# Where the transposes before the last gate stand, which PSUM banks its first token tiles take, and which queue issues the last store

## The chip, the cores and the metric

The kernel runs on one core of one Trainium2 chip. A core has TensorE (PE; its weight loads are listed as PEld), VectorE (DVE), ScalarE (ACT), GpSimd (POOL) and SyncE (SP), which run side by side and wait for each other by semaphores. SP, ACT and POOL also issue DMAs. The metric is the device time of one execution in microseconds (us). It is compared between the kernel before and the kernel after the change.

## What is computed

The reference is one layer of a hybrid decoder trunk over 512 tokens of width 1024, all in float32. The change touches only its last line but one and its last line, the gate on the per-layer embedding and the final norm:

```python
x = x + conv_ffn(rmsnorm(x, ffn_norm), ...)
gate = sigmoid(rmsnorm(x, ple_norm) @ w_ple_gate)     # 512x1024 @ 1024x1024
x = x + gate * (p @ w_ple)
return rmsnorm(x, final_norm)
```

## The kernel before, in words

**Arithmetic.** Each float32 product is made of three matmuls: an operand is split into a high and a low part (`split_into`, L239 on ScalarE and L240 on VectorE; weights by `parts`, L68 on ScalarE and L69 on VectorE), and `mm3` (L204, L205, L206) adds high by high, high by low and low by high into one PSUM bank.

**PSUM.** A bank holds 128 x 512 floats. There are five rotating banks, which the trace calls `mm` (`bank()`), two fixed ones, `sd` (`seeded`), and one small one. A rotating bank is handed out again in the same circular order; whoever gets it waits until its earlier holder has been read for the last time.

**The end of the kernel.** The feed-forward part ends with a down projection (`seven`). While its last steps run on TensorE, some other work is put among them by a list of fillers: the transposes of the second token half (`turn(1, k)`) and products of the embedding with `w_ple` into one `mm` bank, both `sd` banks and another `mm` bank, which ScalarE copies out (L650).

`turn(th, k)` takes one rotating bank, transposes four 128 x 128 blocks of the residual `x` into it on TensorE (L691), and splits the result, scaled by the norm's gain, into an `xe` tile (two instructions L239 on ScalarE, two L240 on VectorE). Four turns make the left operand for the gate of one token half, 256 tokens.

Then the gate loop (L764 on) goes over the four tiles of 128 tokens in the order 2, 3, 0, 1. Tiles 2 and 3 are the second token half, tiles 0 and 1 the first. A tile has 8 steps over the width `k`, each with two groups of three matmuls, one for each half of 512 output columns: 48 matmuls of 512 columns. When its banks are full, sigmoid (L788, in place in the bank), multiply (L789), add (L790), square with row sum (L791, also into the bank) and multiply by the final gain (L792) follow for each half, on ScalarE and VectorE; then the row scale (`rstd_1`, a power on GpSimd at L613), the scaling (L800 on VectorE; for the last half of the last tile L798 on ScalarE) and two stores (L801), all issued by SP. The last tile, 1, is cut into one group of 512 and two of 256 columns.

The gate's weights `wg` are split at the same time as tile 2 runs. Before tile 3, all four turns of the first token half stand in the program text:

```python
for b in (2, 3, 0, 1):
    th, j = divmod(b, 2)
    last = b == 1
    if b == 3:
        for k in range(HK):
            turn(0, k)
```

The scheduler that lays out the instructions of each engine can move an instruction ahead of others; what it made of this text is shown with the change.

Of the kernel before, what the change touches and what calls it, by code (L numbers as in the profile page):

```python
# [14 lines left out]
T = 512  # L15
# [15 lines left out]
HK = KD // 2  # L31
# [13 lines left out]
def trunk(ctx, tc, xT, xr, pT, wsT, par, bsp, w_u0, w_u1, w_v, w_ga, w_gb, w_p, w_pl,  # L45
          w_a, w_b, w_o, w_up, w_dn, w_g, w_ple, gfin, out):
    nc = tc.nc
# [11 lines left out]
    def block(name, shape=(2, T), dtype=F32):  # L59
        return blk.tile([P, *shape], dtype, tag="blk", name=name)  # L60
# [141 lines left out]
    def mm3(o, w, a, first, last, **kw):  # L202
        (wh, wl), (ah, al) = w, a
        PE.matmul(o, wh, ah, start=first, stop=False, **kw)  # L204
        PE.matmul(o, wh, al, start=False, stop=False, **kw)  # L205
        PE.matmul(o, wl, ah, start=False, stop=last, **kw)  # L206
# [10 lines left out]
    def bank():  # L217
        return ps.tile([P, T], F32, tag="mm", name="mm")
# [9 lines left out]
    def split(src, scale=None):  # L228

        b = block("blk", (2, T), F32R)  # L230
        split_into(b, src, scale)
        return b

    def split_into(b, src, scale=None):
        if scale is None:
            S.copy(b[:, 0, :], src)
            V.tensor_tensor(b[:, 1, :], src, b[:, 0, :].bitcast(F32), op=ALU.subtract)  # L237
        else:
            S.activation(b[:, 0, :], src, AF.Copy, scale=scale)  # L239
            V.scalar_tensor_tensor(b[:, 1, :], src, scale, b[:, 0, :].bitcast(F32),  # L240
                                   op0=ALU.mult, op1=ALU.subtract)
# [9 lines left out]
    def col(c, i):  # L251
        return pr[:, c + i:c + i + 1]
# [69 lines left out]
    seeded = [psb.tile([P, T], F32, tag=f"sd{n}", name="sd") for n in range(2)]  # L322
# [123 lines left out]
    for k in range(KD):  # L446
        if k + 1 < KD:
            load(k + 1)
        b = split(x[k], col(C_MIX, k))
# [23 lines left out]
    for f in range(KD):  # L473
# [4 lines left out]
        if f % 2:  # L478
            k = f // 2
# [126 lines left out]
    def rstd_1(sums):  # L606

        ms = small.tile([P, 1], F32, tag="fms", name="fms", bufs=NT)
        V.tensor_scalar(ms, sums[0], 1.0 / D, EPS, op0=ALU.mult, op1=ALU.add)
        for s in sums[1:]:  # L610
            V.scalar_tensor_tensor(ms, s, 1.0 / D, ms, op0=ALU.mult, op1=ALU.add)
        r = small.tile([P, 1], F32, tag="fr", name="fr", bufs=8)
        G.tensor_tensor(r, ms, neghalf[:, :1], op=ALU.pow)  # L613
        return r
# [5 lines left out]
    def columns(z, b, f):  # L620

        return z[b][:, f // HK, f % HK * P:(f % HK + 1) * P]
# [43 lines left out]
    def conv(i, o):  # L666
        cc = work("cc")
        S.activation(cc, o, AF.Identity, scale=col(C_CW, 3 * i + 2), bias=col(C_CB, i))
        V.scalar_tensor_tensor(cc[:, 1:], o[:, :T - 1], col(C_CW, 3 * i + 1), cc[:, 1:],
                               op0=ALU.mult, op1=ALU.add)  # L670
        V.scalar_tensor_tensor(cc[:, 2:], o[:, :T - 2], col(C_CW, 3 * i), cc[:, 2:],
                               op0=ALU.mult, op1=ALU.add)
        return cc
# [12 lines left out]
    def turn(th, k):  # L686
        tp = bank()
        t = block("xe", (2, 2, H), F32R)
        for i, f in enumerate((k, HK + k)):
            for j in range(2):  # L690
                PE.transpose(tp[:, (2 * i + j) * P:(2 * i + j + 1) * P], columns(x, 2 * th + j, f), ident)  # L691
        for i, f in enumerate((k, HK + k)):
            split_into(t[:, i], tp[:, i * H:(i + 1) * H], col(C_PLE, f))
        XE[th].append(t)
# [23 lines left out]
    for i in range(KF):  # L718
# [11 lines left out]
        b = conv(2 * i + 1, o2)  # L730
# [13 lines left out]
        if part:  # L744
            q0, n = part
            last = q0 + n == KF // 2
# [17 lines left out]
    for b in (2, 3, 0, 1):  # L764
        th, j = divmod(b, 2)
        last = b == 1
        if b == 3:
            for k in range(HK):
                turn(0, k)

        if last:
            groups = [[(bank(), 0)], [(bank()[:, :H], T)], [(bank()[:, :H], T + H)]]
        else:
            groups = [[(bank(), 0), (bank(), T)]]
        fss = small.tile([P, 3], F32, tag="fss", name="fss")
        n = 0
        for group in groups:
            for k in range(KD):
                a = XE[th][k % HK][:, k // HK]
                a = [a[:, z, j * P:(j + 1) * P] for z in range(2)]  # L780
                for ob, c0 in group:
                    mm3(ob, a, [z[:, c0:c0 + ob.shape[-1]] for z in wg[k]], k == 0, k == KD - 1)
            for ob, c0 in group:
                w = ob.shape[-1]
                fh, c1 = divmod(c0, T)
                pc = ple[b][:, fh, c1:c1 + w]
                xc = x[b][:, fh, c1:c1 + w]
                S.activation(ob, ob, AF.Sigmoid, scale=r_emb[b])  # L788
                V.tensor_tensor(pc, ob, pc, op=ALU.mult)  # L789
                V.tensor_tensor(xc, xc, pc, op=ALU.add)  # L790
                S.activation(ob, xc, AF.Square, accum_out=fss[:, n:n + 1])  # L791
                V.tensor_tensor(pc, xc, gB[:, c0:c0 + w], op=ALU.mult)  # L792
                n += 1
        r = rstd_1([fss[:, i:i + 1] for i in range(n)])
        for g in range(2):
            ot = ple[b][:, g]
            if g and last:
                S.activation(ot, ot, AF.Copy, scale=r)  # L798
            else:
                V.tensor_scalar_mul(ot, ot, r)  # L800
            nc.sync.dma_start(out[b, :, g * T:(g + 1) * T], ot)  # L801


_ORDER = ["xT", "xr", "pT", "wsT", "par", "bsp", "w_u0", "w_u1", "w_v", "w_ga", "w_gb", "w_p", "w_pl",
# [72 lines left out]
```

## Time and profile before

| what | value |
|---|---|
| time, median of 3 runs | 784.43 us (784.0 to 787.2) |
| the profiled execution: its time | 783.97 us |
| its span in the trace | 782.2 us |
| TensorE busy | 770.5 us, 98% of the span |
| VectorE, ScalarE, GpSimd busy | 532.2, 376.8, 59.9 us |
| chain of work that ended last | TensorE 95% of the span |

The profiled execution's time is 1.77 us more than its span, since the span begins and ends with the first and last instruction in the trace. Times in the trace count from the span's start. L numbers are lines of the kernel before.

### The profile page before, as it was taken

The numbers are of one execution on the slowest core, as the hardware profiler recorded it, in microseconds if no ns is written. First come the engines' busy times: TensorE is split into PE (matmuls) and PEld (weight loads), VectorE is DVE, ScalarE is ACT, GpSimd is POOL, SyncE is SP. The second block draws the span as 40 slices with busy tenths as digits, with TensorE's granted clock in tenths as the row PEclk, the third lists the DMA queues.
The fourth block names the chain that finished last, engine by engine and source line by source line (L and its number), as shares of the span: only waits on it lengthen the run. The fifth ranks groups of instructions, "written<-read, shape, count | busy, mean of one in ns | idle before, by whom it ended". The sixth has DMA issues, their size and how long they took to land.

```text
span 782.2 us, 9301 instructions
## 1 busy us (share of the span) xinstructions
PE 770.5 (98%) x3482; PEld 639.4 (82%) x3482; DVE 532.2 (68%) x748; ACT 376.8 (48%) x542; POOL 59.9 (8%) x97
## 2 busy tenths in 40 slices
PE   9999999999999999999999999999999999999896
PEld 8888878888888888888888888888888888888785
DVE  7795668766566734636576778666668767679735
ACT  5576765582232312325545454544445534458713
POOL 0310200000112100001000000000001010030300
PEclk9999999999999999999999999999999999999998
DMA  9992624224032508101831444732335572383211
GB/s 339 325 229 93 176 81 136 107 97 171 30 109 80 215 27 311 67 0 57 323 113 46 108 108 108 274 131 54 81 109 134 203 196 58 108 185 98 81 54 54
DMA packets 40925, 103.21 MB, mean 132 GB/s; under 512 B 3632, under 2 KB 3760, under 8 KB 40880
## 3 DMA queue, kind: packets, MB, share of 16 engines
q1 hardware_dynamic: 33280, 86.78, 31.9%
q0 software_dynamic: 6016, 11.54, 9.0%
q10 hardware_dynamic: 1584, 4.31, 1.5%
q8 instruction: 27, 0.44, 0.2%
q14 instruction: 18, 0.15, 0.1%
HBM read 99.46 MB, written 3.15 MB: 131 GB/s over the span
## 4 chain that ended last, share of the span: by engine, by line
PE 95%; DVE 2%; DMA 1%; ACT 1%; issue 1%; POOLq 0%; ACTq 0%; DVEq 0%
PE mm L204 25%; PE mm L205 25%; PE mm L206 25%; PE sd L204 6%; PE sd L205 6%; PE sd L206 6%; DMA pt<-in_pT 1%; PE mm L515 1%; PE wake L261 1%; PE mm L628 0%; PE mm L691 0%; ACT whi L68 0%; DVE wlo L69 0%; DVE sg L590 0%; DVE sg L589 0%
## 5 line engine op out<-in xcount | busy, mean ns | idle before, releaser
L69 DVE TENSOR_TENSOR wlo<-raw,whi 128x1024 fp32r<-128x1024 f32 (+1 forms) x186 | 217.9, 1178 | 158.9 <-ACT whi L68 158.4
L68 ACT CAST whi<-raw 128x1024 fp32r<-128x1024 f32 (+1 forms) x179 | 183.8, 1031 | 203.3 <-PE mm L206 59.8
L204 PE MATMUL mm<-blk,whi 128*128 128x512 f32 x480 | 187.3, 391 | 0.0
L205 PE MATMUL mm<-blk,whi 128*128 128x512 f32 x480 | 187.1, 390 | 0.0
L206 PE MATMUL mm<-blk,wlo 128*128 128x512 f32 x480 | 186.6, 389 | 0.0
L204 PEld LDWEIGHTS mm<-blk,whi 128*128 128x128 f32 x480 | 90.3, 188 | 19.1 <-DVE blk L240 0.2
L206 PEld LDWEIGHTS mm<-blk,wlo 128*128 128x128 f32 x480 | 90.2, 188 | 18.8
L205 PEld LDWEIGHTS mm<-blk,whi 128*128 128x128 f32 x480 | 90.3, 188 | 18.5
L204 PE MATMUL mm<-whi,blk 128*128 128x512 f32 x210 | 82.1, 391 | 0.0
L205 PE MATMUL mm<-wlo,blk 128*128 128x512 f32 x210 | 81.8, 389 | 0.0
L206 PE MATMUL mm<-whi,blk 128*128 128x512 f32 x210 | 81.7, 389 | 0.0
L204 PEld LDWEIGHTS mm<-whi,blk 128*128 128x128 f32 x210 | 39.4, 188 | 8.3 <-DVE blk L237 0.2
L206 PEld LDWEIGHTS mm<-whi,blk 128*128 128x128 f32 x210 | 39.4, 188 | 8.2
L205 PEld LDWEIGHTS mm<-wlo,blk 128*128 128x128 f32 x210 | 39.4, 188 | 8.0
L204 PE MATMUL sd<-whi,blk 128*128 128x512 f32 x114 | 44.5, 391 | 0.0
L206 PE MATMUL sd<-whi,blk 128*128 128x512 f32 x114 | 44.4, 389 | 0.0
L205 PE MATMUL sd<-wlo,blk 128*128 128x512 f32 x114 | 44.4, 389 | 0.0
L105 POOL DMA_DIRECT2D raw<-in_w_dn x16 | 18.2, 1241 | 314.9 <-DMA raw<-in_w_dn 205.1
L204 PE MATMUL sd<-whi,cmb 128*128 128x512 f32 x92 | 36.0, 391 | 0.8 <-ACT u L375 0.8
L204 PE MATMUL mm<-whi,cmb 128*128 128x512 f32 x92 | 36.1, 392 | 0.0
L205 PE MATMUL sd<-wlo,cmb 128*128 128x512 f32 x92 | 35.8, 389 | 0.0
L206 PE MATMUL mm<-whi,cmb 128*128 128x512 f32 x92 | 35.8, 389 | 0.0
(171 smaller groups left out, 1080.8 us busy)
## 6 DMA issues: line engine op xcount, KB each, us to landing
raw<-in_w_up SPq DMA_DIRECT2D x44, 512.0 KB, 4.5
raw<-in_w_dn SPq DMA_DIRECT2D x25, 512.0 KB, 3.6
raw<-in_w_dn POOLq DMA_DIRECT2D x12, 512.0 KB, 6.3
raw<-in_w_v SPq DMA_DIRECT2D x10, 512.0 KB, 9.7
raw<-in_w_ga SPq DMA_DIRECT2D x10, 512.0 KB, 4.1
raw<-in_w_gb SPq DMA_DIRECT2D x8, 512.0 KB, 3.6
raw<-in_w_p SPq DMA_DIRECT2D x8, 512.0 KB, 4.5
raw<-in_w_b SPq DMA_DIRECT2D x8, 512.0 KB, 3.9
```

The source lines that it names most:

```text
L68: (V.tensor_copy if first else S.copy)(hi[:, :cols], raw[:, :cols])
L69: V.tensor_tensor(lo[:, :cols], raw[:, :cols], hi[:, :cols].bitcast(F32), op=ALU.subtract)
L105: (G if kw else nc.sync).dma_start(o, block_of(name, ch), **kw)
L204: PE.matmul(o, wh, ah, start=first, stop=False, **kw)
L205: PE.matmul(o, wh, al, start=False, stop=False, **kw)
L206: PE.matmul(o, wl, ah, start=False, stop=last, **kw)
L261: PE.matmul(wake, ones, ones, start=True, stop=True)
L515: PE.matmul(mx[:, n * P:(n + 1) * P], vt[n].rearrange("p a t -> p (a t)")[:, f * P:(f + 1) * P], wsm[:, f, :], start=True, stop=True)
```

## The change

Three things are changed. The four turns of the first token half no longer stand between tile 2 and tile 3; each is written behind one of tile 2's last four steps (`k` = 4 to 7). The first tile of each half (2 and 0, `j == 0`) takes the two `sd` banks and not two rotating ones. And the very last store, the second half of tile 1, is issued by ScalarE, which also makes that half's data, and not by SP. Above the diff's first line everything is as before; from L767 on the lines of the kernel after are lower by up to three (L788 becomes L787, L801 becomes L800).

```diff
     for b in (2, 3, 0, 1):
         th, j = divmod(b, 2)
         last = b == 1
-        if b == 3:
-            for k in range(HK):
-                turn(0, k)
 
         if last:
             groups = [[(bank(), 0)], [(bank()[:, :H], T)], [(bank()[:, :H], T + H)]]
         else:
-            groups = [[(bank(), 0), (bank(), T)]]
+            groups = [[(seeded[0], 0), (seeded[1], T)] if j == 0 else [(bank(), 0), (bank(), T)]]
...
         for group in groups:
...
                 for ob, c0 in group:
                     mm3(ob, a, [z[:, c0:c0 + ob.shape[-1]] for z in wg[k]], k == 0, k == KD - 1)
+                if b == 2 and k >= HK:
+                    turn(0, k - HK)
...
-            nc.sync.dma_start(out[b, :, g * T:(g + 1) * T], ot)
+            (nc.scalar if g and last else nc.sync).dma_start(out[b, :, g * T:(g + 1) * T], ot)
```

On TensorE, the end of tile 2 and the start of tile 3 before the change (`mm<-...,xe` are gate matmuls, `mm<-ident,x` transposes):

```order
L204 MATMUL mm<-whi,xe 128x512 x2
L205 MATMUL mm<-wlo,xe 128x512
L206 MATMUL mm<-whi,xe 128x512
L205 MATMUL mm<-wlo,xe 128x512
L206 MATMUL mm<-whi,xe 128x512
L691 MATMUL mm<-ident,x 128x128 x13
L204 MATMUL mm<-whi,xe 128x512
```

Three of the sixteen transposes had already been moved ahead, into step 3 of tile 2, and stay there in both kernels; the other thirteen stood in one row between the tiles. The same place after the change, from step 6 of tile 2 on:

```order
L691 MATMUL mm<-ident,x 128x128 x4
L204 MATMUL sd<-whi,xe 128x512
L205 MATMUL sd<-wlo,xe 128x512
L206 MATMUL sd<-whi,xe 128x512
L204 MATMUL sd<-whi,xe 128x512
L205 MATMUL sd<-wlo,xe 128x512
L206 MATMUL sd<-whi,xe 128x512
L691 MATMUL mm<-ident,x 128x128 x4
L204 MATMUL mm<-whi,xe 128x512
```

Tile 2 now fills `sd` banks, and the thirteen stand as 1, 4, 4 and 4 behind its steps 4, 5, 6 and 7; tile 3 starts behind the last four.

On ScalarE, from the last weight split on, before the change (the `ACT_TABLE_LOAD` is the one for sigmoid):

```order
L68 CAST whi<-raw 128x1024
L788 ACT_TABLE_LOAD
L788 ACTIVATE mm<-mm,fr 128x512 x2
L239 ACTIVATE xe<-mm,pr 128x256 x3
L791 ACTIVATE mm,fss<-x 128x512 x2
L239 ACTIVATE xe<-mm,pr 128x256 x5
L788 ACTIVATE mm<-mm,fr 128x512 x2
```

And after it:

```order
L239 ACTIVATE xe<-mm,pr 128x256 x5
L787 ACT_TABLE_LOAD
L787 ACTIVATE sd<-sd,fr 128x512
L239 ACTIVATE xe<-mm,pr 128x256 x2
L787 ACTIVATE sd<-sd,fr 128x512
L239 ACTIVATE xe<-mm,pr 128x256
L790 ACTIVATE sd,fss<-x 128x512 x2
L787 ACTIVATE mm<-mm,fr 128x512 x2
```

Most splits of the turned tiles now stand ahead of tile 2's sigmoids; there is one table load in both.

## Rows read from the trace of the kernel before

**Rows 1.** The page: the span, and the granted TensorE clock in 40 slices.

```profile
span 782.2 us, 9301 instructions
...
PEclk9999999999999999999999999999999999999998
```

**Rows 2.** The chain that ended last, 735 to 740 us: start, length, what.

```profile
735.83 0.24 PE mm L206
736.10 0.67 ACT mm L788
...
738.77 0.73 ACT mm L791 x2
739.54 0.66 PE mm L691 x4
```

**Rows 3.** Timeline of TensorE, tiles 2 and 3: start, length, engine, line.

```profile
725.11 0.39 PE L204 MATMUL mm<-whi,xe 128*128 128x512 f32 x1
...
736.35 1.14 PE L691 MATMUL mm<-ident,x 128*128 128x128 f32 x9
739.54 0.66 PE L691 MATMUL mm<-ident,x 128*128 128x128 f32 x4 [2.05 <-ACT mm L791]
740.16 0.50 PE L204 MATMUL mm<-whi,xe 128*128 128x512 f32 x1
...
743.72 0.58 PE L204 MATMUL mm<-whi,xe 128*128 128x512 f32 x1
...
744.37 0.40 PE L206 MATMUL mm<-whi,xe 128*128 128x512 f32 x1
```

**Rows 4.** Three stretches: length, each engine's busy time, granted clock, DMA share, GB/s.

```profile
716.36:720.09 3.73, 3.73 (x25) 3.22 (x24) 3.52 (x10) 2.62 (x7) 0.00 (x0) 1.00 0.00 0
...
736.35:740.16 3.81, 1.76 (x15) 1.32 (x13) 3.31 (x6) 3.44 (x9) 0.00 (x0) 1.00 0.23 83
740.16:744.37 4.21, 4.21 (x12) 3.30 (x12) 3.74 (x11) 1.91 (x5) 0.54 (x1) 0.59 0.30 118
```

**Rows 5.** Timeline of TensorE, two places with transposes among matmuls.

```profile
716.36 1.03 PE L691 MATMUL mm<-ident,x 128*128 128x128 f32 x8
...
717.70 0.39 PE L206 MATMUL mm<-whi,cmb 128*128 128x512 f32 x1
...
729.64 0.49 PE L691 MATMUL mm<-ident,x 128*128 128x128 f32 x3
...
730.90 0.40 PE L204 MATMUL mm<-whi,xe 128*128 128x512 f32 x1
```

**Rows 6.** Instructions that write the turned tiles `xe`: ns min/median/max, first and last start.

```profile
L239 ACT ACTIVATE xe<-mm,pr x16: 471/474/491, 717.0 to 744.3; 128x256 fp32r<-128x256 f32 x16
L240 DVE SCALAR_TENSOR_TENSOR xe<-mm,pr,xe x16: 470/476/484, 717.5 to 744.8; 128x256 fp32r<-128x256 f32 x16
```

**Rows 7.** Timeline of VectorE during tile 2.

```profile
728.16 5.76 DVE L69 TENSOR_TENSOR wlo<-raw,whi 128x1024 fp32r<-128x1024 f32 x5 [0.78 <-ACT whi L68]
```

**Rows 8.** Timeline of ScalarE just before tile 2.

```profile
723.22 1.31 ACT L650 COPY ple<-sd 128x512 f32<-128x512 f32 x2
```

**Rows 9.** Timeline of all engines at the end.

```profile
777.86 0.72 ACT L798 ACTIVATE ple<-ple,fr 128x512 f32<-128x512 f32 x1 [0.91 <-POOL fr L613]
...
778.38 0.81 SPq L801 DMA_DIRECT2D out<-ple  x2
```

**Rows 10.** Two stretches at the end; the last two columns are DMA share and GB/s.

```profile
779.10:779.80 0.70, 0.00 (x0) 0.00 (x0) 0.00 (x0) 0.00 (x0) 0.00 (x0) 0.50 0.86 336
779.80:780.50 0.70, 0.00 (x0) 0.00 (x0) 0.00 (x0) 0.00 (x0) 0.00 (x0) 0.50 1.03 395
```

**Rows 11.** DMA issues, 700 us to the end: queue, count, size, median us to landing.

```profile
out<-ple SPq DMA_DIRECT2D x8, 256.0 KB, 2.2
raw<-in_w_g SPq DMA_DIRECT2D x3, 512.0 KB, 4.7
...
gB<-in_gfin ACTq DMA_DIRECT2D x1, 512.0 KB, 3.9
```

## The prediction

> **What bounds the kernel now.** I read the page first, then the chain of waits at the end of the kernel, then TensorE's timeline around it, and last the windows for its clock. The page has a span of 782.2 us and a granted clock in the top tenth in all 40 slices but the last [rows 1]. TensorE is busy 98% of the span, so time can come back only where it stands still or runs slowly. The chain shows such a place inside the stretch that the change touches. It runs on TensorE to the end of tile 2, leaves it at 736.10 for tile 2's sigmoid, passes through VectorE and the square at 738.77, and comes back to TensorE at 739.54 with the last four transposes [rows 2].
>
> TensorE's timeline says why. After tile 2 it does nine transposes, then stands idle for 2.05 us, and what ended the idle time is a square (L791) [rows 3]. The turns use rotating banks. Five exist; the bank of the fourth turn is one that tile 2 filled, and it comes free only when tile 2's square has been written and read there. So a whole epilogue of a tile lies on the path. A second loss follows: the stretch 736.35 to 740.16 ends with the clock still granted in full, but the next, 740.16 to 744.37, has a mean grant of 0.59, that is, mostly the lower of the two levels, 1.2 GHz instead of 2.4 [rows 4]. In it the matmuls start 0.396 us apart (740.16 to 743.72 are nine steps [rows 3]). At full clock they start 0.227 us apart: the 24 matmuls of steps 4 to 7 of tile 2 take from 730.90 [rows 5] to 736.35 [rows 3], 5.45 us.
>
> **What the place costs now.** Without the thirteen transposes tile 3 would start at 736.35. Its twelfth matmul, at 744.37, lies 8.02 us behind that [rows 3], of which eleven steps at full clock are 2.50. The remaining 5.52 us are transposes, idle time and low clock together.
>
> **What the transposes cost among matmuls.** The trace has them twice. Eight stand at 716.36, where a matmul was due; the third matmul behind them starts at 717.70, 1.34 us later, and two steps are 0.45, so the eight cost 0.89, or 0.111 each. Three stand at 729.64; the fifth matmul behind them starts at 730.90, 1.26 us later, four steps are 0.91, so the three cost 0.35, or 0.117 each [rows 5]. The smaller group is the dearer per piece. For 1, 4, 4 and 4 I take 0.117, or 1.5 us for thirteen. The low bound is 0.111, or 1.4 us; the high one 0.155, or 2.0 us, from the four that took 0.62 us from 739.54 to 740.16 [rows 3], the worst that a row shows. Those already in step 3 cost the same in both kernels.
>
> **The move itself.** With the turns in step with tile 2 and tile 2 out of the rotating banks, no transpose waits for tile 2's epilogue: the four turns get banks whose holders were the turns and embedding products ahead of tile 2. Then 5.52 - 1.5 = 4.0 us come off, and tile 3 starts at 736.35 + 1.5 = 737.85. No gap is left that the clock could fall after. With the bounds it is 3.5 to 4.1 us.
>
> **What the move adds elsewhere.** Eight L239 of 0.474 us and eight L240 of 0.476 us [rows 6] now run beside tiles 2 and 3, 3.8 us on each engine. Their reader is tile 0, which starts a whole tile (48 x 0.227 = 10.9 us) after 737.85, at about 748.7. I cost them at nothing. They cannot hold back the weight splits of tile 2, since on both engines they are queued behind the last of these: VectorE's five end at 733.92 [rows 7]. The order of the last turns' splits and tile 2's sigmoids on ScalarE and VectorE is mixed, but no matmul before tile 0 needs either.
>
> Three new waits are added on banks. (1) Tile 2's first matmul needs the `sd` banks, which ScalarE copies out until 723.22 + 1.31 = 724.53 [rows 8]; it starts at 725.11 [rows 3]. A margin of 0.58 us covers it. Every later gate matmul is queued behind it, so a copy later than that would cost its lateness. (2) Tile 3's second group, at about 738.1, takes the bank of the first turn, whose transposes end at about 732.4. Its two L239 follow, and its two L240 once VectorE is free at 733.92, so it is free by about 735. Margin 3 us. (3) Tile 0 needs tile 2's squares out of `sd`. Before, sigmoid to last square took from 736.10 to 738.77 + 0.73 = 739.50 [rows 2]; that much behind 737.85, plus three splits mixed in, is about 743. Margin 5 us. I cost all three at nothing.
>
> **The last store.** ScalarE ends the data at 777.86 + 0.72 = 778.58; SP issues its two stores in 778.38 to 779.19 [rows 9], the second behind the first. From ScalarE's queue the second can be issued at about 778.6 and not 778.8. But data flow from 779.10 to 780.50 with DMA shares of 0.86 and 1.03 [rows 10], that is, the engines work through both stores without a break. An earlier issue of the second cannot end that stretch sooner by more than a sliver. I take 0. Bounds: a gain of 0.2 us, the issue time; a loss of 1.7, if a store from ScalarE's queue landed as late as the gain load from that queue, 3.9 against 2.2 us. That load had twice the bytes, and loads of its size from SP took 4.7 [rows 11], which speaks for 0.
>
> The Trainium skill (Trainium Kernel Development and Optimization, Key Constraints) says that queues of all issuing engines run on the same 16 DMA engines and that issuing from several only saves issue time. By that rule the store would give 0.2 us. This trace agrees that no more can be had, and its full DMA shares say less.
>
> **The sum.** 783.97 (the profiled execution) - 4.0 = 780.0 us; with the bounds of transposes and a gain at the store, 779.7 to 780.5. The profiled execution was 0.46 us below the median of the runs shown, 784.43, so a median could stand at 780.0 to 780.4; I say 780.1. That is 0.5% under the median, just where a change can be told from none (about 0.5%, 3.9 us).
>
> **The rivals.**
> 1. *The wait goes, the clock still falls once* near the mixed stretch. For it: the low stretch came 3.8 us after the last matmul of tile 2, and transposes were part of those 3.8 us. Against it: the 16 transposes at 716 to 720, in two groups of eight with six matmuls between, had a grant of 1.00 [rows 4]. The price is that of the low stretch: 9 x (0.396 - 0.227) = 1.5 us there, with its edges 2, so about 782.
> 2. *Slower: the transposes themselves bring the clock down*, from step 4 of tile 2 until tile 3 has run a while. At half clock a matmul costs 0.17 more and a transpose 0.04: 24 x 0.17 + 13 x 0.04 + 9 x 0.17 = 6.1 us, so about 786. It decides from 4.0 / 0.17 = 24 slow matmuls on. Speaking against it are the same rows at 716 to 720: the grant was 1.00 with a higher share of transposes. The Trainium skill (TensorE: Matmul & The Clock Gate, Part 4) says that the full clock does not engage for transposes. By that page this rival would come true; this trace disagrees where it can be seen.
> 3. *The wait moves to tile 3's second bank*. If the first turn's splits came 5 us late, behind something that I take to be early, TensorE would wait 2 us there and lose the clock again: about 784, no change. Against it stands the margin of 3 us.
> 4. *ScalarE's store lands late*: 780.0 + 1.5 = 781.5.
>
> **How the numbers follow.** My forecast has a chance of 0.75, rival 1 0.10, rival 2 0.04, rival 3 0.06, rival 4 0.05. The predicted time is 780.1. The forecast's own range, 779.7 to 780.5 from the profiled time, gets half a microsecond either way for the spread between runs; rivals 4 and 1 reach to 782. So 779.0 to 782.2 leaves out rivals 2 and 3 and about a tenth more. Within the forecast, the line of 0.5% (784.43 - 3.92 = 780.5) is passed about 77 times in 100: 0.75 x 0.77 = 0.58 for faster. The rest of it, with rivals 1, 3 and 4, is 0.38 for the same, and rival 2 is 0.04 for slower.
>
> **What would show it.** In the changed profile: no idle time of TensorE between tiles 2 and 3; a grant of 1.00 from 725 to the end of tile 1; tile 3's first matmul at 737.8 to 738.4; the end of tile 1 four microseconds earlier; the stretch from the last matmul to the span's end as long as now. A wait of TensorE at 725 for L650, one at 738 for L240, or a grant under 1.00 behind 731 would prove a step wrong, and a last stretch longer than now would point to the store.

## The result and the profile after

The kernel after took 779.76 us (median of 6 runs, 778.97 to 780.61) against 784.68 us before (6 runs, 783.35 to 787.2). The ratio is 0.9932, 95% interval 0.9914 to 0.995, that is, 3.9 to 6.7 us less. The predicted time was 780.1 us.

The page of the kernel after: the span, busy times and the granted clock in 40 slices.

```profile
span 777.2 us, 9296 instructions
...
PE 767.3 (99%) x3482; PEld 637.0 (82%) x3482; DVE 532.9 (69%) x748; ACT 376.9 (48%) x542; POOL 62.2 (8%) x97
...
PEclk9999999999999999999999999999999999999998
```

TensorE's timeline of the kernel after, from tile 2's first matmul to tile 3's start: start, length, engine, line.

```profile
724.08 0.39 PE L204 MATMUL sd<-whi,xe 128*128 128x512 f32 x1
...
731.25 0.27 PE L691 MATMUL mm<-ident,x 128*128 128x128 f32 x1
...
732.75 0.60 PE L691 MATMUL mm<-ident,x 128*128 128x128 f32 x4
...
734.58 0.60 PE L691 MATMUL mm<-ident,x 128*128 128x128 f32 x4
...
736.41 0.60 PE L691 MATMUL mm<-ident,x 128*128 128x128 f32 x4
736.76 0.48 PE L204 MATMUL mm<-whi,xe 128*128 128x512 f32 x1
737.08 0.39 PE L205 MATMUL mm<-wlo,xe 128*128 128x512 f32 x1
```

The idle time and the slow matmuls of [rows 3] are gone: tile 3 starts 0.35 us after the last transposes began (736.41 to 736.76). The same stretches as windows of the kernel after; the columns are those of [rows 4].

```profile
736.00:740.00 4.00, 4.00 (x21) 3.33 (x20) 2.48 (x6) 3.68 (x7) 0.00 (x0) 1.00 0.10 36
740.00:745.00 5.00, 5.00 (x23) 4.14 (x23) 4.18 (x10) 1.55 (x5) 0.54 (x1) 1.00 0.00 0
```

TensorE is busy throughout and the grant is 1.00, where before it was 0.59 [rows 4]. The end of the kernel after, all engines:

```profile
772.85 0.72 ACT L797 ACTIVATE ple<-ple,fr 128x512 f32<-128x512 f32 x1 [0.91 <-POOL fr L613]
...
773.37 0.33 SPq L800 DMA_DIRECT2D out<-ple  x1
773.60 0.35 ACTq L800 DMA_DIRECT2D out<-ple  x1
```

Two lengths tell the parts of the kernel apart, and all that follows uses them. The first runs from tile 2's first matmul to tile 1's last sigmoid, which starts when the last matmul has ended; the second from there to the span's end. The last sigmoid of before, then of after:

```profile
775.04 0.45 ACT L788 ACTIVATE mm<-mm,fr 128x256 f32<-128x256 f32 x1 [0.97 <-PE mm L206]
```

```profile
770.03 0.45 ACT L787 ACTIVATE mm<-mm,fr 128x256 f32<-128x256 f32 x1 [0.97 <-PE mm L206]
```

| profile | tile 2's first matmul | last sigmoid | first length | second length |
|---|---|---|---|---|
| before | 725.11 | 775.04 | 49.93 | 7.16 |
| after | 724.08 | 770.03 | 45.95 | 7.17 |
| difference | 1.03 | | 3.98 | -0.01 |

So 4.0 us come from the stretch that the change touches, nothing from the end, and 1.0 us was there before tile 2 starts, where both kernels have the same instructions. That last part is looked at below.

### The profile page after: what moved, and what is told of

The parts are those of the page before. It is cut to its first block, busy times and chain, and to the rows that moved or that the text cites. A ratio compares the mean times of both kernels' runs of the same rounds, so it can differ in the third digit from the quotient of the medians.

```text
span 777.2 us, 9296 instructions
## 1 busy us (share of the span) xinstructions
PE 767.3 (99%) x3482; PEld 637.0 (82%) x3482; DVE 532.9 (69%) x748; ACT 376.9 (48%) x542; POOL 62.2 (8%) x97
## 4 chain that ended last, share of the span: by engine, by line
PE 97%; DVE 1%; ACT 1%; DMA 0%; issue 0%; POOLq 0%; ACTq 0%
PE mm L204 25%; PE mm L205 24%; PE mm L206 24%; PE sd L204 7%; PE sd L205 7%; PE sd L206 7%; PE mm L515 1%; PE mm L628 0%; PE mm L691 0%; DMA pr<-in_par 0%; ACT whi L68 0%; DVE wlo L69 0%; DVE sg L590 0%; PE ss L298 0%; ACT ple L797 0%
## 5 line engine op out<-in xcount | busy, mean ns | idle before, releaser
L204 PE MATMUL sd<-whi,cmb 128*128 128x512 f32 x92 | 36.0, 391 | 0.8 <-ACT u L375 0.8
L206 PE MATMUL sd<-whi,cmb 128*128 128x512 f32 x92 | 35.8, 389 | 0.0
```

## The experiments

The first four runs are compared with the same 24 further runs of the kernel before.

**Each of the two moves alone.** The first run only puts tiles 2 and 0 in the `sd` banks.

```diff
-            groups = [[(bank(), 0), (bank(), T)]]
+            groups = [[(seeded[0], 0), (seeded[1], T)] if j == 0 else [(bank(), 0), (bank(), T)]]
```

> Only tiles 2 and 0 move to the two sd banks; the turns stay in one row between tiles 2 and 3. Measure: from tile 2's first matmul to the last sigmoid, 49.93 us in the profile before and 45.95 in the one after. Theory A (the loss was the wait for tile 2's bank and the low clock behind it): the turns get other banks, no idle time, 45.9 to 46.1, time 4 us below before (ratio 0.995). Rival B (it was the row of thirteen transposes, and only spreading them among the steps keeps TensorE fast): some 2 us of the 4 stay, 48 us or more, with a grant under 1.00 behind the row.

Measured: 779.96 us (7 runs) against 783.50 (24 runs of before), ratio 0.9965 (0.9951 to 0.998). First length 770.16 - 724.29 = 45.87 us. TensorE's timeline between tiles 2 and 3:

```profile
735.56 1.58 PE L691 MATMUL mm<-ident,x 128*128 128x128 f32 x13
736.89 0.48 PE L204 MATMUL mm<-whi,xe 128*128 128x512 f32 x1
```

All thirteen transposes stand in one row and cost 1.33 us to the next matmul's start. There is no wait, and theory A holds: spreading them is not what brings the time back. Rival B falls. The ratio is nearer 1 than the 0.995 expected, for a reason that the later runs show; one of the seven runs, not profiled, took 782.35 us at a mean grant of 0.996, where the others have 0.997 to 0.999.

The second run only moves the turns.

```diff
-        if b == 3:
-            for k in range(HK):
-                turn(0, k)
...
+                if b == 2 and k >= HK:
+                    turn(0, k - HK)
```

> Only the turns move among tile 2's steps; tiles 2 and 0 stay in rotating banks. The built program gives the fourth turn the bank of the first turn and tile 3 those of the second and third. Theory A: the first turn's splits end early enough (about 735 on the time scale of before), so no wait of note, 45.9 to 46.4 us from tile 2's first matmul to the last sigmoid, ratio 0.995. Rival C (the fixed banks are what takes the wait away): a wait of TensorE for a bank at the end of tile 2 or in tile 3, 48 us or more.

Measured: 780.38 us (5 runs) against 783.50, ratio 0.9963 (0.9951 to 0.9975). First length 771.54 - 725.50 = 46.04 us; no idle time of TensorE. The end of tile 2 on TensorE:

```profile
737.84 0.60 PE L691 MATMUL mm<-ident,x 128*128 128x128 f32 x4
738.19 0.48 PE L204 MATMUL mm<-whi,xe 128*128 128x512 f32 x1
```

Theory A holds again. Written among tile 2's steps, the fourth turn gets a bank that an earlier turn has given back, and not one of tile 2's, so the wait for the epilogue goes just as well. So the order in which banks are handed out is not always circular, as the description of the kernel before has it: a bank that tile 2 still holds was passed over here, and in a strict circle this run would have waited. Rival C falls. Either move alone takes the whole loss away; in the kernel after, one of them is enough and the other costs nothing that can be seen.

**The store alone.**

```diff
-            nc.sync.dma_start(out[b, :, g * T:(g + 1) * T], ot)
+            (nc.scalar if g and last else nc.sync).dma_start(out[b, :, g * T:(g + 1) * T], ot)
```

> Only the last store moves to ScalarE's queue. Theory A: the DMA engines carry both stores in one piece anyway, so from the last sigmoid to the span's end 7.1 to 7.2 us as before (7.16), ratio 1.000, and 49.9 us from tile 2's first matmul to the last sigmoid. Rival (the issue time counts): 0.2 us less at the end. Rival (a store from that queue lands late): up to 1.7 us more.

Measured: 783.51 us (12 runs) against 783.50, ratio 1.0002 (0.9992 to 1.0012). First length 775.30 - 725.36 = 49.94, second 782.5 - 775.30 = 7.2 us. The DMA issues of its last 4.5 us: queue, count, size, median us to landing.

```profile
out<-ple SPq DMA_DIRECT2D x1, 256.0 KB, 2.0
out<-ple ACTq DMA_DIRECT2D x1, 256.0 KB, 2.4
```

ScalarE issues its store 0.24 us behind the start of SP's (778.87 and 778.63), where SP took 0.81 us for issuing two [rows 9]; but the store then takes longer to land (2.4 us) than those from SP did (2.2 [rows 11]). The DMA engines are full in this run too, with a share of 1.06 from 779.80 to 780.50, so an earlier issue most likely only waits there; that the second length stays at 7.2 us fits. The interval of the times, 0.6 us to one side and 0.9 to the other, is too wide for a gain of 0.2, so this rests on the second length.

**Wait and clock apart.** The kernel before, with nine matmuls that nobody reads ahead of the fourth turn. They are extra work; nothing is left out.

```diff
+    def fillers(n=9):
+        o = pst.tile([P, T], F32, tag="st", name="fil")
+        for i in range(n):
+            PE.matmul(o, XE[1][0][:, 0, 0, :P], wg[KD - 1][0][:, :T], start=True, stop=True)
...
             for k in range(HK):
+                if k == HK - 1:
+                    fillers()
                 turn(0, k)
```

> The kernel before, with nine matmuls of 512 columns whose result nobody reads put into the idle time ahead of the fourth turn; the wait for the bank stays. It parts the loss into wait and clock. Theory A (the clock fell because TensorE stood idle): grant 1.00 throughout, tile 3's first matmul as late as before, but then at 0.227 us apart, 47.9 to 48.1 us from tile 2's first matmul to the last sigmoid, so 2 us of the 4 come back, ratio 0.9975. Rival D (transposes bring the clock down, not the idle time): grant under 1.00 as before, 49.9 us or more.

Measured: 782.43 us (11 runs) against 783.50, ratio 0.999 (0.9981 to 0.9998). First length 772.66 - 724.23 = 48.43 us. TensorE's timeline:

```profile
736.38 2.30 PE L768 MATMUL fil<-whi,xe 128*128 128x512 f32 x9
738.68 0.65 PE L691 MATMUL mm<-ident,x 128*128 128x128 f32 x4
739.29 0.50 PE L204 MATMUL mm<-whi,xe 128*128 128x512 f32 x1
739.62 0.39 PE L205 MATMUL mm<-wlo,xe 128*128 128x512 f32 x1
739.86 0.39 PE L206 MATMUL mm<-whi,xe 128*128 128x512 f32 x1
740.09 0.40 PE L204 MATMUL mm<-whi,xe 128*128 128x512 f32 x1
```

The window behind the gap:

```profile
740.00:745.00 5.00, 5.00 (x24) 3.96 (x23) 3.92 (x11) 1.80 (x4) 0.54 (x1) 1.00 0.27 105
```

The wait is as it was: the last four transposes start 14.45 us behind tile 2's first matmul, and 14.43 before. With useless work in the gap, tile 3's matmuls start 0.23 to 0.24 us apart from the second on, and the grant is 1.00, where the kernel before has 0.59 [rows 4]. All eleven runs have a mean grant of 0.997 to 0.999. So the idle time, and not the transposes by themselves, lowers the clock, and rival D falls. But 1.5 us came back (49.93 - 48.43) where I had expected 2: of the 3.98 us the wait is 2.48 and the clock 1.5. The wait costs more than its idle time of 2.05 us. Of the 0.43 us between them, 0.26 are the four transposes, which take 0.61 us to the next matmul's start behind a wait, at full clock too, against 0.35 in the kernel after (736.41 to 736.76); the rest was not taken apart.

Its runs also come out only 1.1 us under those of before by the medians. The next runs say why.

**The kernel before, three more times.** The 24 runs of before in these comparisons fall into two groups by their mean grant: 15 at 0.995 (782.97 to 784.5 us) and 9 at 0.997 or 0.998 (781.29 to 782.64, one at 783.68). Three further profiles were taken, with no edit; a run beside them, not profiled, took 781.77 us at 0.998.

> The kernel before once more, for a second profile of it. Its runs fall into two groups, mean grant 0.995 near 783.7 us and 0.997 to 0.998 near 781.7. Theory A: they differ by whether the clock falls behind the idle time ahead of the fourth turn; in a run of the first group 49.9 us from tile 2's first matmul to the last sigmoid and a low stretch behind 740, in one of the second 48.4 and none. Rival: they differ at the start, where the clock rises, and the low stretch behind the idle time is in all.

> As the run before it: a further profile of the kernel before, 49.9 us with a low stretch behind the idle time, or 48.4 without one.

> As the two runs before it: a further profile of the kernel before, 49.9 us with a low stretch behind the idle time, or 48.4 without one.

| profile of before | time | mean grant | grant 740 to 745 | first length |
|---|---|---|---|---|
| first of the three | 783.46 | 0.995 | 0.68 | 774.53 - 724.58 = 49.95 |
| second | 782.10 | 0.997 | 1.00 | 773.17 - 724.76 = 48.41 |
| third | 784.51 | 0.995 | 0.66 | 775.61 - 725.67 = 49.94 |

The second one has the idle time too, but its clock did not fall. Its timeline and then its window; compare [rows 3, 4]:

```profile
739.20 0.66 PE L691 MATMUL mm<-ident,x 128*128 128x128 f32 x4 [2.05 <-ACT mm L791]
739.82 0.50 PE L204 MATMUL mm<-whi,xe 128*128 128x512 f32 x1
740.15 0.40 PE L205 MATMUL mm<-wlo,xe 128*128 128x512 f32 x1
740.39 0.40 PE L206 MATMUL mm<-whi,xe 128*128 128x512 f32 x1
```

```profile
740.00:745.00 5.00, 5.00 (x22) 3.98 (x22) 4.44 (x13) 2.17 (x5) 0.54 (x1) 1.00 0.27 105
```

So the same idle time of 2.05 us lowers the clock in some executions and not in others, and that is the 1.5 us between 49.94 and 48.41. The rival on record, that the groups differ at the start only, falls. What decides in which execution the clock falls was not found. By the groups, an estimate since most of these runs have no profile, it fell in some 15 of 24 runs of before. The run with the fillers never pays it, so against a mixture it gains about two thirds of 1.5 us, which agrees with 1.1. By the first lengths the change gains 2.5 us against an execution in which the clock did not fall, and 4.0 against one in which it did. In the shares of the 24 runs that is 3.4 us, which lies in the intervals of both moves alone (1.6 to 3.8 and 2.0 to 3.8 us).

**Transposes alone.** The kernel after with 64 transposes that nobody reads behind the last turn. They are extra work.

```diff
+        if b == 3:
+            o = pst.tile([P, T], F32, tag="st", name="fil")
+            for i in range(64):
+                PE.transpose(o[:, i % NT * P:(i % NT + 1) * P], columns(x, 3, i % KD), ident)
```

> The kernel after, with 64 transposes whose result nobody reads in one row behind the last turn, between tiles 2 and 3. Theory A (transposes alone keep TensorE at the higher clock; only idle time lowers it): grant 1.00 through the row and behind it, 0.109 to 0.117 us each, so 7.0 to 7.5 us more than the 45.95 us from tile 2's first matmul to the last sigmoid, 53.0 to 53.4. Rival 2 of the prediction (transposes bring the clock down): a grant near 0.5 within the row or behind it, and 54.5 us or more.

Measured: 786.78 us (one run), first length 777.86 - 724.91 = 52.95 us, 7.00 more than the kernel after, 0.109 each. The windows of this run, and its row of transposes in the timeline:

```profile
736.00:744.00 8.00, 8.00 (x69) 7.69 (x68) 5.88 (x12) 5.87 (x12) 0.00 (x0) 1.00 0.13 45
744.00:750.00 6.00, 6.00 (x32) 5.07 (x31) 1.15 (x4) 0.14 (x2) 0.54 (x1) 1.00 0.24 90
```

```profile
737.68 7.15 PE L770 MATMUL fil<-ident,x 128*128 128x128 f32 x64
744.59 0.48 PE L204 MATMUL mm<-whi,xe 128*128 128x512 f32 x1
```

The grant is 1.00 in the row and behind it. The Trainium skill (TensorE: Matmul & The Clock Gate, Part 4) says that the full clock does not engage for transposes. Here 68 of them in one row, some 7.3 us, kept a clock that was up, in the one execution that was taken. Whether transposes alone would raise a low clock was not tried.

## Why the prediction was right

**The wait for tile 2's bank** was the loss, and it went. Predicted from the profiled pair: 4.0 us, with bounds of 3.5 to 4.1; measured on the same two lengths: 3.98. Tile 3 starts 736.76 - 724.08 = 12.68 us behind tile 2's first matmul; predicted 737.85 - 725.11 = 12.74. That the path is the one predicted, the bank of tile 2 and no other, is shown by the first run: it only takes tile 2 out of the rotating banks, and the whole wait goes.

**The transposes** were priced at 1.5 us for thirteen. In the kernel after, the rows at 736.41 and 737.08 give the four: 0.67 us to the second matmul behind, less one step of 0.227, is 0.44, or 0.11 each. The high bound of 0.155 was the price of four behind a wait, and none among matmuls. Rival 2's 0.04 more for a transpose at half clock seems to be 0.155 less 0.111, which takes that row for the low clock's, though the window up to 740.16 has a grant of 1.00 [rows 4].

**The three new bank waits** cost nothing, as argued: no wait of TensorE shows from 724.08 to the last matmul. For the first, ScalarE's copies out of the `sd` banks end at 723.50, 0.58 us ahead of tile 2's first matmul, the margin that was predicted. For the second, the first three L240 of the turned tiles, with both of the first turn among them, are over by 734.77, and tile 3's fourth matmul starts at 737.54. For the third, tile 2's last square ended at 743.31 in the kernel after, where tile 0 starts at 747.76; so the 5 us of margin were 4.5. In that last estimate the prediction read 739.50 as the end of tile 2's last square. It is the first half's; the second half's starts at 739.40 and ends at 739.98, so the stretch was some half a microsecond longer than it took. The margin covers that. VectorE's row of the splits and ScalarE's timeline, both of the kernel after:

```profile
733.89 0.88 DVE L240 SCALAR_TENSOR_TENSOR xe<-mm,pr,xe 128x256 fp32r<-128x256 f32 x2 [0.59 <-ACT xe L239]
```

```profile
736.08 1.28 ACT L787 ACT_TABLE_LOAD   x1
...
742.58 0.60 ACT L790 ACTIVATE sd<-x 128x512 f32<-128x512 f32 x1 [1.63 <-DVE x L789]
743.12 0.19 ACT L790 ACTIVATION_READ_ACCUMULATOR sd<-x 128x1 f32 x1
```

**The store** at 0 was right: the second length is 7.17 us against 7.16, and its run alone gives 1.0002 with 7.2 us.

**What I had not seen** is that the low clock behind the idle time is no fixed cost. I took it as part of every execution, since the profiled one had it. Over the 24 runs of before it is paid in about two thirds, so the change's worth is 2.5 us in some and 4.0 in others, and the moves alone measured 3.1 and 3.5 us by the medians. The predicted time does not suffer from this, since the loss was taken off the time of the very execution that had it; from the second of the three profiles the same sum, 782.10 less 2.5, would have come to 779.6. The gain does. The forecast gain was 784.43 - 780.1 = 4.3 us, and the first comparison gives 4.9 us. About 1 us of the pair of profiles lies ahead of tile 2. Nearly all of that is there at the start already, as the same two matmuls of before and of after show.

```profile
5.11 0.80 PE L204 MATMUL mm<-blk,whi 128*128 128x512 f32 x1
...
10.80 0.39 PE L204 MATMUL mm<-blk,whi 128*128 128x512 f32 x1
```

```profile
4.99 0.50 PE L204 MATMUL mm<-blk,whi 128*128 128x512 f32 x1 [0.25 <-ACT whi L68]
...
9.94 0.39 PE L204 MATMUL mm<-blk,whi 128*128 128x512 f32 x1
```

The first matmuls of the profile before run slowly for longer, and at the 22nd it is 0.86 us behind. Over the ten profiles, whose programs are the same up to there, tile 2's first matmul starts anywhere from 724.08 (after) to 725.67 (before, the third of three), and profiles of before lie at 724.58 to 725.67. So this part is spread between executions, and no effect of the change was shown in it. With a spread of 1.1 us among profiles of one kernel, hitting the measured median to 0.3 us was in part luck. Whether the rest of the 4.9 us is more than such spread stays open; its interval begins at 3.9.

**The line of 0.5%.** The first comparison puts the change at 0.5 to 0.86%, each move alone at 0.2 to 0.5%, and by the lengths it is 2.5 to 4.0 us, 0.3 to 0.5%. The prediction's 0.58 to 0.38 for the two sides of the line fits a change that stands so close to it.

No version tried is clearly better than the kernel after: with either move alone the first length is 45.87 and 46.04 us, against 45.95. What is left in it, at full clock, is matmuls and 1.8 us of transposes that have to be made.

## What to carry to other kernels

Where an instruction on the bound engine waits at the end of a tile, look which buffer it got and who held it last. Here one bank of five, held through a tile's epilogue up to the first half's square, cost 2.5 us, and it went as well by giving the tile other banks as by asking for the buffers earlier, where they then came from another holder; an engine that is busy 98% of the span still has such places. A gap on TensorE can have a second price behind it, the slow matmuls until the clock is back, here 1.5 us in some executions, and useless matmuls in the gap took that part away. A single profile shows one draw of that price: read the mean grant of many runs before putting it in a sum.

## What the runs showed of the hardware that was not expected

- The same idle time of 2.05 us, at the same place, was followed by the low clock in three profiles of before (783.97, 783.46 and 784.51 us) and in that with the store moved, and not in a fourth of before (782.10 us). The difference is 1.5 us.
- 68 float32 transposes of 128 x 128 in one row took 0.109 us each and kept the grant at 1.00 (one execution).
- Four transposes behind a wait take 0.61 to 0.62 us to the next matmul's start at full clock, against 0.35 among matmuls.
